# A convolution summed in PSUM, and weight low parts split between two engines, in a two-layer encoder trunk on one core

## The chip, the cores and the metric

The kernel runs as one program on one core of a Trainium2 chip. The metric is device time in microseconds (us), the median of 3 runs. The engines are named as in the profile: PE is the matrix engine (PEld its weight loads), DVE the vector engine, ACT the scalar engine, POOL is GpSimd, and SP issues most DMA transfers.

## What is computed

Two layers over a 256 x 2048 residual `h`, in float32:

```python
for i in range(DEPTH):                      # 2
    hn = _rmsnorm(h, norm_g[i])
    u = hn @ w_in[i]                        # 2048 -> 3*1024 + 1024 + 2*256 + 1024
    a_val, a_glu, a_z, q, k, v, b_z = jnp.split(u, offs, axis=-1)
    ya = _conformer_conv(a_val, a_glu, ...) # a = val*sigmoid(glu); depthwise conv, 31 taps;
                                            # layernorm over 1024 channels; silu
    ya = ya * jax.nn.silu(a_z)
    yb = _window_attention(q, k, v, bias_band, sink[i]) * jax.nn.silu(b_z)   # 16 heads
    h = h + jnp.concatenate([ya, yb], axis=-1) @ w_out[i]
    e = _rmsnorm(p[i] @ w_pe[i], pe_g[i])
    h = h + e * jax.nn.sigmoid(h @ w_pg[i])
return _rmsnorm(h, final_g)
```

## The kernel before

Everything is held transposed: channels on the 128 partitions, the 256 positions along the free axis. The weights stream from HBM in "halves" of 128 x 1024 numbers, two halves to a 1 MB transfer (`raw`, 3 buffers). Each matrix product is made of three products of the PE's rounded format, so every half is split first into a high part and a low part (`split`, L163 and L166): ACT casts `raw` to the high part, and DVE subtracts it from `raw` to give the low part. Both parts are one tile `w` (5 buffers); below, w9 is the tile of half 9. A half occupies PE with 24 matmuls of 256 columns: for each of 8 blocks high x high (L394), high x low of the activations (L395), and low x high (L396). L396 is the first that needs the low part. A layer has 154 halves, numbered from 0 in layer 0 and from 154 in layer 1; within a layer they serve `w_pe` (0 to 3), the convolution's value and gate columns `ag` (4 to 35), keys and values (36 to 43), attention gates and queries `zb`, `q` (44 to 75), the convolution's output gate `za` (76 to 91), then `w_out` and `w_pg`.

DVE, PE and ACT run their instructions in the order in which the program records them (`MAN`); POOL's are put in order by the scheduler. After each half `pump` records some convolution taps (about three, by `RATES`) and one piece of each side task. Halves are split four ahead of their use, but only two or so ahead in the first few halves of a layer, where halves come in pairs that PE uses interleaved (4 with 5, 6 with 7, 8 with 9, 10 with 11), while DVE still makes the normalised activations (`hn` L463, then `hg` L467).

The convolution of one tile of 128 channels (`conv`) is one ACT instruction for the middle tap and the bias (L553), and 30 multiply-adds on DVE (L560), each of which reads the input `a` and the sum `acc`, both in SBUF. Two tiles are worked on in turn, so that neighbouring instructions belong to different tiles. When a tile is done, POOL adds it to `ysum` (L565).

The side task `attention` runs for 8 pairs of heads, one after the other, while halves 54 to 91 are used: it loads its bias (`load_bias`, L334, a DMA that POOL issues), PE makes the scores (`sc`, L629), DVE adds the bias and takes the row limits (L635), ACT the exponentials (L642), DVE the denominators `den` (L646 and L647; both inputs of L646 are in SBUF), ACT scales (L650), PE transposes (`pt`, L656) and multiplies with the values (`av`, L666). Another side task, `embed`, has ACT square `e` (L380) and POOL add the squares to `eacc` (L381) during halves 16 to 31.

Of the kernel before, what the change touches and what calls it, by code (L numbers as in the profile page):

```python
# [10 lines left out]
F32 = mybir.dt.float32  # L11
F32R = mybir.dt.float32r
AF = mybir.ActivationFunctionType
ALU = mybir.AluOpType
PSUM = bass.MemoryType.PSUM
DRAM = bass.MemoryType.DRAM

P = 128
D = 2048
S = 256  # L20
# [10 lines left out]
PAD = TAPS // 2  # L31
# [17 lines left out]

NB_FIRST = 14  # L50
NSPL = 5
MAN = 'DVE,PE,Activation'
LY = (2, 1)
ORD = 1
AW = (0,0,0,0)
# [61 lines left out]
NHALF = len(HALVES)  # L117
# [3 lines left out]
PO_CW, PO_CB, PO_LG, PO_LB, PO_PE = 0, TAPS * NCT, (TAPS + 1) * NCT, (TAPS + 2) * NCT, (TAPS + 3) * NCT  # L121
# [4 lines left out]
def trunk_kernel(ctx: ExitStack, tc: tile.TileContext, xT, pT, wst, par, gain, relb, sinkp, onehot, out):  # L126
    nc = tc.nc
    ET = mybir.EngineType
    if MAN:
        ctx.enter_context(tc.manual_schedule(engines={getattr(ET, x) for x in MAN.split(",")}))  # L130
    big = ctx.enter_context(tc.tile_pool(name="big", bufs=5))
# [1 line left out]
    wspl = ctx.enter_context(tc.tile_pool(name="wspl", bufs=NSPL))  # L133
    cst = ctx.enter_context(tc.tile_pool(name="cst", bufs=1))
    wk = ctx.enter_context(tc.tile_pool(name="wk", bufs=2))
    ps = ctx.enter_context(tc.tile_pool(name="ps", bufs=8, space=PSUM))
    dram = ctx.enter_context(tc.tile_pool(name="dram", bufs=1, space=DRAM))

    def bigt(name, dt=F32):

        return big.tile([P, 2, 8, S], dt, tag="big", name=name)

    def halves(t):
        return [t[:, 0], t[:, 1]]
# [14 lines left out]
    def split(h):  # L159
        raw = raws[h // 2][:, h % 2, :]  # L160
        w = wspl.tile([P, 2, HALF], F32R, tag="w", name=f"w{h}")
        hi, lo = w[:, 0], w[:, 1]
        nc.scalar.copy(hi, raw)  # L163
        spl[h] = w
        if h not in (4, 5):
            nc.vector.tensor_sub(lo, raw, hi.bitcast(F32))  # L166

    def first_lo(h):

# [3 lines left out]
    def ahead(h):  # L173

        while state["spl"] < min(h, TOT - 1):
            n = state["spl"] + 1
            while state["raw"] < min(n // 2 + LD - 1, TOT // 2 - 1):
                state["raw"] += 1
                load(state["raw"])
            if HALVES[n % NHALF][0] != "w_pe" or n >= NHALF:  # L180
                split(n)
            state["spl"] = n

    def get(h):

        r = h % NHALF
        if r < 12:
            ahead(h + (r | 1) + 2 - r)
        else:
            ahead(h + LS)  # L190
        return spl.pop(h)
# [82 lines left out]
    h = halves(bigt("x"))  # L274
# [18 lines left out]
    def pcol(l, o):  # L293
        return pars[:, l * PW + o:l * PW + o + 1]
# [111 lines left out]
    class Cursor:  # L406
        h = 0
# [39 lines left out]
    for l in range(DEPTH):  # L447
# [27 lines left out]
        for q in range(4):  # L475
            n = Cursor.h
            Cursor.h += 1
            if l:
                w = get(n).rearrange("p t (j k c) -> p t j k c", j=4, k=2)
            else:  # L480
                raw = raws[n // 2][:, n % 2, :].rearrange("p (j k c) -> p j k c", j=4, k=2)
# [65 lines left out]
        a, acc = halves(bigt(f"ac{l}"))  # L547
# [2 lines left out]

        def conv(t, l=l, a=a, acc=acc, ysum=ysum, done=done):
            w = lambda k: pcol(l, PO_CW + t * TAPS + k)
            nc.scalar.activation(acc[:, t, :], a[:, t, :], AF.Identity, bias=pcol(l, PO_CB + t), scale=w(PAD))  # L553
            yield
            for k in range(TAPS):
                s = k - PAD
                if s == 0:
                    continue
                lo_, hi_ = max(0, -s), min(S, S - s)
                nc.vector.scalar_tensor_tensor(acc[:, t, lo_:hi_], a[:, t, lo_ + s:hi_ + s], w(k),  # L560
                                               acc[:, t, lo_:hi_], ALU.mult, ALU.add)
                yield
            done.append(t)
            if 2 <= len(done) <= NCT - 2:
                nc.gpsimd.tensor_add(ysum, acc[:, done[0], :] if len(done) == 2 else ysum, acc[:, t, :])  # L565

        def glu(t, b):
            u = wk.tile([P, S], F32, name=f"u{l}_{t}", tag="sg")
            nc.scalar.activation(u, b[:, 1, :], AF.Sigmoid)
            nc.vector.tensor_mul(a[:, t, :], b[:, 0, :], u)  # L570
            conv_q.append(conv(t))
# [27 lines left out]
        for q in range(4):  # L599
            n = Cursor.h  # L600
            Cursor.h += 1
            w = get(n).rearrange("p t (k c) -> p t k c", k=4)
            for kk in range(4):
                k = 4 * q + kk
# [66 lines left out]
        for i in range(0, 8, 2):  # L671
# [6 lines left out]
            for hh in range(2):  # L678
                r, o = rows_of[hh], rows_of[1 - hh]
# [158 lines left out]
        h = e  # L838
# [10 lines left out]
    for j in (0, 2, 12, 4, 6, 14, 8, 10):  # L849
        for x in [slice(0, 1), slice(1, 2)] if j == 0 else [slice(0, 2)]:  # L850
            d = og[j // 8][:, j % 8:j % 8 + 2, :][:, x, :]
            eng, r = (nc.gpsimd, rbs) if j >= 12 else (nc.vector, rb)
# [81 lines left out]
```

## Time and profile before

| | |
|---|---|
| median of 3 runs | 983.94 us (983.38 to 984.1) |
| the profiled execution's own time | 983.99 us |
| its span, first to last instruction | 982.2 us |
| mean granted PE clock | 0.992 |
| PE busy (matmuls) | 965.8 us, 98% of the span |
| PEld busy | 925.5 us, 94% |
| DVE busy | 774.6 us, 79% |
| ACT busy | 560.0 us, 57% |
| POOL busy | 86.6 us, 9% |

How to read it: busy time is the time in which an engine had an instruction under way, over one profiled execution. The page also follows a chain of work back from the last instruction, lists what each engine waited for, and shows stretches of the timeline row by row.

### The profile page before, as it was taken

How to read it: one execution, taken by the hardware profiler on the slowest of the kernel's cores; microseconds unless marked ns; L12 is line 12 of the kernel's file. 1: busy time of each engine (PE TensorE's matmuls, PEld its weight loads, DVE VectorE, ACT ScalarE, POOL GpSimd, SP SyncE). 2: the span in 40 equal slices, each digit the busy share in tenths (PEclk: the TensorE clock that was granted, in tenths of full speed). 3: DMA queues.
4: the chain of work that ended last, by engine and by line, in shares of the span. 5: the costliest groups of instructions: out<-in, count | busy, mean ns of one | idle time of the engine just before them, and what ended most of it. 6: DMA issues, size and time to landing. Idle time of an engine off the chain costs nothing.

```text
span 982.2 us, 18152 instructions
## 1 busy us (share of the span) xinstructions
PE 965.8 (98%) x7438; PEld 925.5 (94%) x7438; DVE 774.6 (79%) x1319; ACT 560.0 (57%) x862; POOL 86.6 (9%) x87
## 2 busy tenths in 40 slices
PE   8999999999999999999999999999999999999994
PEld 7999999999999999988899999999999999998884
DVE  4899989987787576687789998988887867667763
ACT  4655454777875554455566444568778545446551
POOL 0022001010000000011103200000100000100111
PEclk9999999999999999999999999999999999999997
DMA  7764636555544466446556555456454445654522
GB/s 287 254 238 171 213 131 215 189 178 181 166 153 177 149 238 225 172 172 230 198 184 237 175 203 181 172 188 204 146 168 165 172 143 200 217 191 162 197 104 86
DMA packets 29135, 182.49 MB, mean 186 GB/s; under 512 B 3723, under 2 KB 4284, under 8 KB 9212
## 3 DMA queue, kind: packets, MB, share of 16 engines
q1 hardware_dynamic: 24284, 165.17, 47.2%
q0 software_dynamic: 3472, 12.88, 4.4%
q10 hardware_dynamic: 1296, 3.28, 0.9%
q8 instruction: 58, 0.95, 0.4%
q14 instruction: 25, 0.20, 0.1%
HBM read 177.09 MB, written 4.23 MB: 185 GB/s over the span
## 4 chain that ended last, share of the span: by engine, by line
PE 97%; DVE 1%; DMA 1%; ACT 0%; POOL 0%; issue 0%; DVEq 0%; SPq 0%; ACTq 0%
PE g L391 12%; PE o L394 6%; PE o L395 6%; PE o L396 6%; PE ag L396 6%; PE ag L394 6%; PE ag L395 6%; PE g L392 6%; PE za L394 3%; PE zb L394 3%; PE q L394 3%; PE q L395 3%; PE zb L395 3%; PE za L395 3%; PE zb L396 3%; PE q L396 3%
## 5 line engine op out<-in xcount | busy, mean ns | idle before, releaser
L166 DVE TENSOR_TENSOR w<-raw,w 128x1024 fp32r<-128x1024 f32 x306 | 372.3, 1227 | 119.1 <-ACT w L163 116.1
L163 ACT CAST w<-raw 128x1024 fp32r<-128x1024 f32 x308 | 316.2, 1047 | 180.2 <-PE ag L396 45.1
L560 DVE SCALAR_TENSOR_TENSOR ac<-ac,pars 128x241 f32<-128x241 f32 (+11 forms) x480 | 217.9, 503 | 1.0
L391 PE MATMUL g<-h,w 128*128 128x512 f32 x496 | 175.3, 399 | 0.0
L396 PE MATMUL ag<-hg,w 128*128 128x256 f32 x512 | 145.2, 284 | 0.5 <-DVE w L166 0.5
L394 PE MATMUL ag<-hg,w 128*128 128x256 f32 x512 | 145.5, 284 | 0.0
L395 PE MATMUL ag<-hg,w 128*128 128x256 f32 x512 | 145.1, 283 | 0.1
L392 PE MATMUL g<-h,w 128*128 128x256 f32 x496 | 139.3, 281 | 0.0
L391 PEld LDWEIGHTS g<-h,w 128*128 128x128 f32 x496 | 93.2, 188 | 23.1
L394 PEld LDWEIGHTS ag<-hg,w 128*128 128x128 f32 x512 | 98.3, 192 | 0.9 <-ACT ac L553 0.9
L396 PEld LDWEIGHTS ag<-hg,w 128*128 128x128 f32 x512 | 98.3, 192 | 0.8 <-DVE w L166 0.7
L395 PEld LDWEIGHTS ag<-hg,w 128*128 128x128 f32 x512 | 98.3, 192 | 0.3 <-DVE hg L467 0.3
L392 PEld LDWEIGHTS g<-h,w 128*128 128x128 f32 x496 | 93.8, 189 | 0.0
L394 PE MATMUL za<-hg,w 128*128 128x256 f32 x256 | 73.7, 288 | 0.0
L394 PE MATMUL o<-yb,w 128*128 128x256 f32 x256 | 73.4, 287 | 0.0
L394 PE MATMUL q<-hg,w 128*128 128x256 f32 x256 | 73.3, 286 | 0.0
L394 PE MATMUL zb<-hg,w 128*128 128x256 f32 x256 | 73.2, 286 | 0.0
L395 PE MATMUL o<-yb,w 128*128 128x256 f32 x256 | 72.6, 284 | 0.0
L396 PE MATMUL o<-ya,w 128*128 128x256 f32 x256 | 72.5, 283 | 0.0
L394 PE MATMUL o<-ya,w 128*128 128x256 f32 x256 | 72.5, 283 | 0.0
L395 PE MATMUL o<-ya,w 128*128 128x256 f32 x256 | 72.5, 283 | 0.0
L396 PE MATMUL o<-yb,w 128*128 128x256 f32 x256 | 72.5, 283 | 0.0
(229 smaller groups left out, 2192.9 us busy)
## 6 DMA issues: line engine op xcount, KB each, us to landing
raw<-in_wst SPq DMA_DIRECT2D x153, 1024.0 KB, 4.9
bias<-fscr POOLq DMA_DIRECT2D x16, 384.0 KB, 3.8
raw<-in_wst SPq DMA_DIRECT2D x5, 512.0 KB, 9.8
x<-in_xT ACTq DMA_DIRECT2D x4, 512.0 KB, 7.1
hx<-in_xT POOLq DMA_DIRECT2D x8, 256.0 KB, 3.6
hscr<-e POOLq DMA_DIRECT2D x2, 1024.0 KB, 4.9
hx<-hscr POOLq DMA_DIRECT2D x8, 256.0 KB, 3.4
out_t<-og ACTq DMA_DIRECT2D x4, 256.0 KB, 3.0
```

The lines of the kernel that those rows point to most:

```text
L163: nc.scalar.copy(hi, raw)
L166: nc.vector.tensor_sub(lo, raw, hi.bitcast(F32))
L391: nc.tensor.matmul(o, w[:, 0], x, start=start, stop=False, skip_group_check=True)
L392: nc.tensor.matmul(o[:, 1], w[:, 1], x[:, 0], start=False, stop=stop, skip_group_check=True)
L394: nc.tensor.matmul(o, w[:, 0], x[:, 0], start=start, stop=False, skip_group_check=True)
L395: nc.tensor.matmul(o, w[:, 0], x[:, 1], start=False, stop=False, skip_group_check=True)
L396: nc.tensor.matmul(o, w[:, 1], x[:, 0], start=False, stop=stop, skip_group_check=True)
L560: nc.vector.scalar_tensor_tensor(acc[:, t, lo_:hi_], a[:, t, lo_ + s:hi_ + s], w(k), acc[:, t, lo_:hi_], ALU.mult, ALU.add)
```

## The change

The sums of the convolution move from `acc` (SBUF) to `y`, a half of one PSUM bank that is set aside for them: the two tiles in work use its two halves. The pool of PSUM banks that all else shares goes from 8 to 7. When a tile's taps are done, a new ACT copy brings `y` to `acc`. In halves 8 to 91 of each layer the low parts of three halves in four are made on POOL instead of DVE (63 subtractions a layer). And POOL joins the engines whose order is the program's.

```diff
-MAN = 'DVE,PE,Activation'
+MAN = 'DVE,PE,Activation,Pool'
...
-    ps = ctx.enter_context(tc.tile_pool(name="ps", bufs=8, space=PSUM))
+    ps = ctx.enter_context(tc.tile_pool(name="ps", bufs=7, space=PSUM))
+
+    cps = ctx.enter_context(tc.tile_pool(name="cps", bufs=1, space=PSUM))
+    ybank = cps.tile([P, 2, S], F32, name="y")
...
         nc.scalar.copy(hi, raw)
         spl[h] = w
         if h not in (4, 5):
-            nc.vector.tensor_sub(lo, raw, hi.bitcast(F32))
+            r = h % NHALF
+            (nc.gpsimd if 8 <= r < 92 and r % 4 else nc.vector).tensor_sub(lo, raw, hi.bitcast(F32))
...
         def conv(t, l=l, a=a, acc=acc, ysum=ysum, done=done):
             w = lambda k: pcol(l, PO_CW + t * TAPS + k)
-            nc.scalar.activation(acc[:, t, :], a[:, t, :], AF.Identity, bias=pcol(l, PO_CB + t), scale=w(PAD))
+            y = ybank[:, t % 2, :]
+            nc.scalar.activation(y, a[:, t, :], AF.Identity, bias=pcol(l, PO_CB + t), scale=w(PAD))
             yield
...
-                nc.vector.scalar_tensor_tensor(acc[:, t, lo_:hi_], a[:, t, lo_ + s:hi_ + s], w(k),
-                                               acc[:, t, lo_:hi_], ALU.mult, ALU.add)
+                nc.vector.scalar_tensor_tensor(y[:, lo_:hi_], a[:, t, lo_ + s:hi_ + s], w(k), y[:, lo_:hi_],
+                                               ALU.mult, ALU.add)
                 yield
+            nc.scalar.copy(acc[:, t, :], y)
             done.append(t)
```

What the change does to the order is seen at three places. The first is DVE at the opening of layer 0's projection, from the low part of half 8 on (w are the split tiles, hn and hg the activations). Before:

```order
L166 TENSOR_TENSOR w8_324<-raw4_201,w8_324 128x1024
L166 TENSOR_TENSOR w9_327<-raw4_201,w9_327 128x1024
L463 SCALAR_TENSOR_TENSOR hn_378<-x_84,gains_100,rh0b_211 128x256 x2
L463 SCALAR_TENSOR_TENSOR hn_382<-x_84,gains_100,rh0b_211 128x256 x2
L467 TENSOR_TENSOR hg0_1_311<-hn_378,hg0_1_311 128x512
L467 TENSOR_TENSOR hg0_1_311<-hn_382,hg0_1_311 128x512
L166 TENSOR_TENSOR w10_390<-raw5_251,w10_390 128x1024
L166 TENSOR_TENSOR w11_393<-raw5_251,w11_393 128x1024
```

and of the change:

```order
L170 TENSOR_TENSOR w8_328<-raw4_205,w8_328 128x1024
L467 SCALAR_TENSOR_TENSOR hn_382<-x_88,gains_104,rh0b_215 128x256 x2
L467 SCALAR_TENSOR_TENSOR hn_386<-x_88,gains_104,rh0b_215 128x256 x2
L471 TENSOR_TENSOR hg0_1_315<-hn_382,hg0_1_315 128x512
L471 TENSOR_TENSOR hg0_1_315<-hn_386,hg0_1_315 128x512
```

The low parts of halves 9, 10 and 11 are gone from DVE, and the activations follow w8 at once.

The second is POOL from the column of layer 0's first norm (rh0col) on. Before:

```order
L348 TENSOR_TENSOR rh0col_194<-rh0v_192,mhalf_114 128x2
L751 DMA hx_4032<-in_xT 128x512
L751 DMA hx_4034<-in_xT 128x512
L751 DMA hx_4092<-in_xT 128x512
L327 DMA fscr_128<-fs_553 16x511
L334 DMA bias0_1904<-fscr_128 128x2x384
L334 DMA bias1_2060<-fscr_128 128x2x384
L381 TENSOR_TENSOR eacc_132<-eacc_132,sq_686 128x512
```

and of the change:

```order
L352 TENSOR_TENSOR rh0col_198<-rh0v_196,mhalf_118 128x2
L170 TENSOR_TENSOR w9_331<-raw4_205,w9_331 128x1024
L170 TENSOR_TENSOR w10_394<-raw5_255,w10_394 128x1024
L170 TENSOR_TENSOR w11_397<-raw5_255,w11_397 128x1024
L170 TENSOR_TENSOR w13_456<-raw6_326,w13_456 128x1024
L170 TENSOR_TENSOR w14_519<-raw7_392,w14_519 128x1024
L170 TENSOR_TENSOR w15_522<-raw7_392,w15_522 128x1024
L331 DMA fscr_132<-fs_557 16x511
L170 TENSOR_TENSOR w17_563<-raw8_451,w17_563 128x1024
L170 TENSOR_TENSOR w18_596<-raw9_517,w18_596 128x1024
L170 TENSOR_TENSOR w19_627<-raw9_517,w19_627 128x1024
L385 TENSOR_TENSOR eacc_136<-eacc_136,sq_690 128x512
```

Low parts now fill POOL, and the early loads of the residual (hx) and of the first two biases have moved behind them, to the place where the program records them.

The third is DVE where it makes the first softmax denominators (den_1937 before, den_1945 of the change; ac0 and y are the convolution's sums), with the low part of half 60 ahead of them. Before:

```order
L560 SCALAR_TENSOR_TENSOR ac0_259<-ac0_259,pars_105 128x249
L560 SCALAR_TENSOR_TENSOR ac0_259<-ac0_259,pars_105 128x255
L166 TENSOR_TENSOR w60_2031<-raw30_1875,w60_2031 128x1024
L646 TENSOR_TENSOR den_1937<-den_1937,es_1938 128x4
L647 RECIPROCAL den_1937<-den_1937 128x4
L560 SCALAR_TENSOR_TENSOR ac0_259<-ac0_259,pars_105 128x250
```

and of the change:

```order
L565 SCALAR_TENSOR_TENSOR y_78<-ac0_263,pars_109,y_78 128x249
L565 SCALAR_TENSOR_TENSOR y_78<-ac0_263,pars_109,y_78 128x255
L170 TENSOR_TENSOR w60_2039<-raw30_1883,w60_2039 128x1024
L652 TENSOR_TENSOR den_1945<-den_1945,es_1946 128x4
L653 RECIPROCAL den_1945<-den_1945 128x4
L565 SCALAR_TENSOR_TENSOR y_78<-ac0_263,pars_109,y_78 128x250
```

Half 60's low part stays on DVE, directly ahead of the denominators; the taps read and write y instead of ac0, and half 61's low part is on POOL, beside them.

## Rows read from the trace of the kernel before

**Rows 1.** The page: busy time by engine, share of the span, instructions

```profile
PE 965.8 (98%) x7438; PEld 925.5 (94%) x7438; DVE 774.6 (79%) x1319; ACT 560.0 (57%) x862; POOL 86.6 (9%) x87
```

**Rows 2.** What PE waited for: total us, times, longest; five rows in all

```profile
PE e L490 <- DMA raw<-in_wst: 2.2, 1, 2.2
...
PE ag L396 <- DVE w L166: 0.5, 1, 0.5
```

**Rows 3.** Stretches: length; busy us of PE, PEld, DVE, ACT, POOL; clock

```profile
64.31:75.83 11.52, 11.52 (x99) 11.52 (x98) 11.52 (x18) 5.53 (x7) 4.02 (x3) 1.00 0.55 196
170.00:296.00 126.00, 126.00 (x1046) 121.08 (x1047) 106.20 (x240) 95.86 (x182) 8.54 (x10) 1.00 0.52 176
```

**Rows 4.** Groups by form: busy us, mean ns, idle before

```profile
L381 POOL TENSOR_TENSOR hacc<-hacc,sq 128x512 f32<-128x512 f32 x12 | 15.5, 1291 | 179.0 <-ACT sq L380 179.0
L463 DVE SCALAR_TENSOR_TENSOR hn<-x,gains,rh0b 128x256 f32<-128x256 f32 x16 | 6.7, 475 | 0.0
```

**Rows 5.** Timeline of POOL: start, us, instruction, idle before

```profile
162.25 0.81 POOL L565 TENSOR_TENSOR ysum<-ysum,ac 128x256 f32<-128x256 f32 x1 [7.42 <-DVE ac L560]
```

**Rows 6.** Timeline of ACT, DVE and POOL around two additions of POOL

```profile
86.66 1.70 POOL L381 TENSOR_TENSOR eacc<-eacc,sq 128x512 f32<-128x512 f32 x1 [4.73 <-ACT sq L380]
87.13 0.41 DVE L570 TENSOR_TENSOR ac<-ag,u 128x256 f32<-128x256 f32 x1
...
91.38 0.63 ACT L380 ACTIVATE sq<-e 128x512 f32<-128x512 f32 x1
92.15 1.53 POOL L381 TENSOR_TENSOR eacc<-eacc,sq 128x512 f32<-128x512 f32 x1 [3.79 <-ACT sq L380]
92.44 1.51 DVE L560 SCALAR_TENSOR_TENSOR ac<-ac,pars 128x249 f32<-128x249 f32 x1
```

**Rows 7.** Timeline at halves 8 to 11: ACT, DVE, PE

```profile
34.05 1.99 ACT L163 CAST w<-raw 128x1024 fp32r<-128x1024 f32 x2
35.13 2.36 DVE L166 TENSOR_TENSOR w<-raw,w 128x1024 fp32r<-128x1024 f32 x2 [0.26 <-ACT w L163]
37.84 0.28 PE L396 MATMUL ag<-hg,w 128*128 128x256 f32 x1
39.62 1.99 ACT L163 CAST w<-raw 128x1024 fp32r<-128x1024 f32 x2
43.60 0.28 PE L396 MATMUL ag<-hg,w 128*128 128x256 f32 x1
```

**Rows 8.** Timeline at halves 164 and 165 (8 and 9 of layer 1)

```profile
511.35 2.00 ACT L163 CAST w<-raw 128x1024 fp32r<-128x1024 f32 x2
515.24 0.28 PE L396 MATMUL ag<-hg,w 128*128 128x256 f32 x1
```

**Rows 9.** Timeline of DVE: two taps of one tile in a row

```profile
525.77 0.47 DVE L560 SCALAR_TENSOR_TENSOR ac<-ac,pars 128x242 f32<-128x242 f32 x1
526.27 0.47 DVE L560 SCALAR_TENSOR_TENSOR ac<-ac,pars 128x243 f32<-128x243 f32 x1
```

**Rows 10.** Timeline of the first attention of layer 0, from half 60's split

```profile
182.16 1.99 ACT L163 CAST w<-raw 128x1024 fp32r<-128x1024 f32 x2
183.23 1.22 DVE L166 TENSOR_TENSOR w<-raw,w 128x1024 fp32r<-128x1024 f32 x1 [1.23 <-ACT w L163]
184.37 0.15 DVE L646 TENSOR_TENSOR den<-den,es 128x4 f32<-128x4 f32 x1
184.83 1.71 ACT L650 ACTIVATE s<-s,den 128x256 f32<-128x256 f32 x4 [0.69 <-DVE den L647]
188.01 0.27 PE L656 MATMUL pt<-ident,s 128*128 128x128 f32 x1
```

**Rows 11.** Timeline of the last attention of layer 0

```profile
285.33 1.71 ACT L650 ACTIVATE s<-s,den 128x256 f32<-128x256 f32 x4 [0.69 <-DVE den L647]
288.71 0.27 PE L656 MATMUL pt<-ident,s 128*128 128x128 f32 x1
```

**Rows 12.** The page: DMA issues of POOL, KB each, us to landing

```profile
bias<-fscr POOLq DMA_DIRECT2D x16, 384.0 KB, 3.8
```

## The prediction

> **What bounds the kernel now.** I read the page's busy times first, then what PE waited for, then stretches of the timeline. PE is busy 98% of the span and its weight loads 94%, DVE 79%, POOL 9% [rows 1]. The list of PE's waits has five rows, of 2.2 us down to 0.5 [rows 2]; they lie at the start, in the first halves and at the very end. So from the first tiles of the projection to the last gate PE never stands still: four halves take 11.52 us, 2.88 each, all of it busy at the full granted clock [rows 3]. Nothing that relieves DVE can shorten that. The change can only leave PE's time alone or put gaps into it, and the work is to find where a low part or a result comes later than PE wants it.
>
> **The change part by part.**
>
> *Price of a subtraction on POOL.* The trace before has none of 128 x 1024. Left alone, POOL adds two 128 x 256 operands in 0.81 us [rows 5] and two 128 x 512 in 1.29 [rows 4]: 1.875 ns a column and 0.33 fixed, so 1,024 columns take 0.33 + 1.92 = 2.25 us, against 1.22 on DVE [rows 10]. Below, it could not be less than DVE's 1.22; above, 3.47, if each also stood behind one 1.22 us subtraction of DVE. I take 2.25, the line through POOL's own rows.
>
> *Who holds up whom.* DVE's tap that overlaps POOL's addition at 92.15 takes 1.51 us instead of 0.47: it stood still for 1.04, nearly all of a 512-column addition. Its two inputs are both in SBUF. The multiplication at 87.13, with one input in PSUM and one in SBUF, ran in 0.41 in the middle of another addition of POOL [rows 6]. So taps that read `y` in PSUM should run beside POOL, and what still collides with POOL are DVE's subtractions and other operations with both inputs in SBUF; one that loses to a low part on POOL waits up to its 1.92 us of columns.
>
> *Steady projection.* Three low parts are 6.75 us, with two additions to `eacc` (2.58) 9.3, in 11.52 us for four halves: hidden by the four halves of lead. Without that cover it costs the overflow, from 2.98 us a subtraction on while the squares run, from 3.84 elsewhere. DVE loses 63 x 1.22 = 77 us a layer.
>
> *Taps.* The two tiles now share a bank, so each tap follows the one just before it instead of the last but one. Dependent taps start 0.50 apart [rows 9], of which 0.47 is the tap. DVE has room: in 126 us it is busy 106.2 [rows 3], and sheds 24 x 1.22 = 29. That PSUM is written instead of SBUF is in no row; reading it costs nothing (`hn` with one operand in PSUM takes 475 ns [rows 4]). I take 0, with 0.36 more per tap as the bound: some 100 taps in that stretch would then eat the (126 - 106 + 29 - 12) us that stay free.
>
> *New copies, `ysum`, moved DMAs, one bank less.* An ACT copy per tile (8 a layer) and POOL's addition to `ysum` behind it now make POOL wait for the last tap, with the next low parts queued behind; the lead of 11.52 us covers some us of that, and ACT is busy 95.9 of 126 in its fullest stretch [rows 3]. The bias loads stand behind up to three low parts: 6.75 + 3.8 to land [rows 12] = 10.6, still inside the lead, and DVE wants them only after the scores. The residual's loads start with the first of 14 halves of `w_out`, 40 us before use. Seven banks suffice for `w_out`'s seven sums, and the norm's two small results come before the last of these is begun. All 0.
>
> *The opening of each projection: no cover.* Halves 8 to 11 are split just in time. The cast of w9 ends at 34.05 + 1.99 = 36.04; POOL starts 0.14 after ACT (91.38 + 0.63 to 92.15 [rows 6]); + 2.25 = 38.43. PE wants it at 37.84 [rows 7]: **0.6 late**. In layer 1: 511.35 + 2.00 + 0.14 + 2.25 = 515.74 against 515.24 [rows 8]: **0.5 late**. Nothing later gives this back, since PE has no slack after it. Then w10 and w11 follow each other on POOL: 40.6 + 0.14 + 4.5 = 45.2 against 43.60 [rows 7] + 0.6, 1.0 late if the casts stay; but the order shows `hn` right behind w8 on DVE, without w9's subtraction (1.1), and these casts follow the casts of `hg`. So they move up by as much: 0, with 1.0 a layer as the other end.
>
> *Softmax.* `den` stands right behind half 60's subtraction on DVE (183.23 + 1.22 = 184.45), and half 61's cast ends at 182.16 + 1.99 = 184.15 [rows 10]. So now POOL stands ready with w61 at 184.29 and takes over as DVE's subtraction ends; `den`, two inputs in SBUF, waits 1.92. ACT's scaling ended at 186.54, PE wanted it at 188.01: 1.47 to spare, **0.45 lost**. The last attention of the layer has 288.71 - 287.04 = 1.67 to spare [rows 11]: **0.25 lost**. The six between have more than one hold. 0.7 a layer, 1.4 in all, with 0 as the other end if the short operation slips in first. The Trainium skill, SBUF — State Buffer, section "Who interferes with whom", says that a vector instruction with two SBUF inputs and a GpSimd one that reads SBUF exclude each other for the whole instruction, whichever issues first. By that rule the loss is the full hold and the sum is the one below; by the row of the blocked tap alone, where a tap was the later one, an operation that is earlier would lose nothing and the sum is 985.0.
>
> *Sum.* 983.99 + 1.1 + 1.4 = 986.5 against the profiled execution, which is 0.05 over the median of 983.94: **986.4**.
>
> **The rivals.** What a measurement can tell from no change is about 0.2%, 1.97 us: 981.97 to 985.91.
>
> *Only the openings are late* (the other side: not slower). Place: `den` at halves 60 and 88. If DVE gets it done before POOL starts, the 1.4 falls away: 985.0. For it: the instruction takes 0.15 us. Against: w61 waits for the same moment. It decides from 0.77 us of softmax loss downward.
>
> *The change does nothing that PE sees.* It needs POOL to subtract in under 1.6 us, to be in time at 37.84: 983.9. Against it are both of POOL's rows; for it, only that no row has this shape.
>
> *POOL is the bottleneck of the openings.* At 3.47 a subtraction (the rounded output type dearer, or DVE in the way): w9 1.8, w165 1.7; the second pairs, with casts 1.1 earlier, 39.5 + 0.14 + 6.94 = 46.6 against 43.60 + 1.8, so 1.2 in each layer; softmax 1.4: 7.3 in all, 991.2. In the squares' stretch 3 x 3.47 + 2.58 = 13.0 in 11.52 adds a backlog of 6 over 16 halves, inside the lead. The Trainium skill, GPSIMD Engine Reference, section "Engine selection", keeps two-input elementwise work on VectorE, because GpSimd is about twice as slow. By twice DVE's 1.22 an estimate from that page is 2.45 us, 0.2 more at each opening, 986.8.
>
> *DVE late with taps or with a bias.* PSUM as target dearer by over 0.36 a tap, or a bias row that lands after its scores: every attention then stalls PE, 992 and more. Against it is DVE's free time.
>
> *Faster.* A wait of PE on DVE would have to vanish; the only one is 0.5 [rows 2], in the first halves, whose low parts the change leaves on DVE. Under 982 I see no path.
>
> **How the numbers follow.** Openings and softmax (985.6 to 987.8): 0.52, of which 0.43 over 985.91. Openings only: 0.20, same. Nothing: 0.06, same. POOL dear: 0.13, slower. Taps or bias late: 0.06, slower. Faster: 0.03. Together slower 0.62, same 0.35 and faster 0.03. The range runs from 984.5, just under the openings alone, to 991, the bound of POOL's price; the likeliest case's own is 985.6 to 987.8.
>
> **What would show it.** Right: POOL busy about 86.6 + 126 x 2.25 = 370 us; subtractions of 2.2 to 2.4; two new waits of PE (L400, on POOL) near 38 and 515, of about half a us; waits of PE at `pt` (L662), on ACT, near 188 and 289, and `den` starting some 2 us after the subtraction ahead of it; taps near 0.47, unblocked; DVE less busy by over 100 us. Wrong: subtractions over 3 us, waits of L400 all through the projection, scores waiting for bias, or PE's list of waits unchanged.

## The result, and the profile after

The changed kernel takes 988.84 us (median of 5 runs, 988.37 to 989.24), the kernel before 983.94 in the same series: a ratio of 1.0049, with a 95% interval of 1.0035 to 1.0063. It is slower by 4.9 us. The profiled execution took 989.24 us, with a span of 987.5 at a mean granted clock of 0.993; before, 983.99 and 982.2.

The page after, busy time by engine, to be read against [rows 1]:

```profile
PE 969.5 (98%) x7438; PEld 926.5 (94%) x7438; DVE 713.0 (72%) x1193; ACT 562.5 (57%) x878; POOL 383.4 (39%) x213
```

DVE lost 62 us and POOL gained 297, and PE is still busy 98% of a longer span. What PE waited for, after (total us, times, longest):

```profile
PE ag L400 <- POOL w L170: 1.3, 2, 0.7
...
PE pt L662 <- ACT s L656: 0.6, 2, 0.3
```

These two rows are new against [rows 2]: POOL's low part at L400, once in each layer's opening, and the scaled scores at the transposes `pt`, once in the fourth attention of each layer. Now the first opening, from ACT's, POOL's and PE's timelines, to be read against [rows 7]:

```profile
33.99 2.00 ACT L166 CAST w<-raw 128x1024 fp32r<-128x1024 f32 x2
36.06 2.48 POOL L170 TENSOR_TENSOR w<-raw,w 128x1024 fp32r<-128x1024 f32 x1 [16.29 <-ACT w L166]
38.60 0.39 PE L400 MATMUL ag<-hg,w 128*128 128x256 f32 x1 [0.68 <-POOL w L170]
38.41 2.00 ACT L166 CAST w<-raw 128x1024 fp32r<-128x1024 f32 x2
39.53 4.79 POOL L170 TENSOR_TENSOR w<-raw,w 128x1024 fp32r<-128x1024 f32 x2 [0.98 <-ACT w L166]
```

The cast of w9 ends where it did, POOL starts behind it and ends at 38.54, and PE, which wanted the low part at 37.84, goes on at 38.60. The casts of w10 and w11 moved from 39.62 up to 38.41, and POOL has both low parts done at 44.32, when PE is about to want them. In layer 1 the same matmul, at 515.24 before [rows 8], starts like this:

```profile
518.04 0.38 PE L400 MATMUL ag<-hg,w 128*128 128x256 f32 x1 [0.58 <-POOL w L170]
```

The second kind of loss is in the attentions. In the first one of layer 0, the rows of ACT, DVE, POOL and PE here answer to [rows 10]:

```profile
183.03 1.99 ACT L166 CAST w<-raw 128x1024 fp32r<-128x1024 f32 x2
184.10 1.23 DVE L170 TENSOR_TENSOR w<-raw,w 128x1024 fp32r<-128x1024 f32 x1 [3.35 <-ACT w L166]
185.11 2.48 POOL L170 TENSOR_TENSOR w<-raw,w 128x1024 fp32r<-128x1024 f32 x1 [4.22 <-ACT w L166]
185.25 2.36 DVE L652 TENSOR_TENSOR den<-den,es 128x4 f32<-128x4 f32 x1
187.91 1.71 ACT L656 ACTIVATE s<-s,den 128x256 f32<-128x256 f32 x4 [2.89 <-DVE den L653]
188.90 0.92 PE L662 MATMUL pt<-ident,s 128*128 128x128 f32 x5
191.92 1.15 DVE L645 TENSOR_TENSOR es<-nm,sinkt 128x4 f32<-128x4 f32 x1
```

`den`'s addition of 128 x 4 numbers takes 2.36 us instead of 0.15: it ends as POOL's subtraction ends, 2.2 later. ACT's wait for it grew from 0.69 to 2.89, and the next small addition of the same kind, `es`, is blocked as well.

The fourth attention loses most, and a second part of the change has a share in it, the new copy:

```profile
224.07 0.35 ACT L568 COPY ac<-y 128x256 f32<-128x256 f32 x1
224.97 0.57 ACT L558 ACTIVATE y<-ac,pars 128x256 f32<-128x256 f32 x1 [0.55 <-DVE y L565]
229.64 2.37 DVE L652 TENSOR_TENSOR den<-den,es 128x4 f32<-128x4 f32 x1
233.62 0.33 PE L662 MATMUL pt<-ident,s 128*128 128x128 f32 x1 [0.32 <-ACT s L656]
```

Before, ACT ran the next tile's first tap there as soon as the exponentials were done:

```profile
222.67 0.59 ACT L553 ACTIVATE ac<-ac,pars 128x256 f32<-128x256 f32 x1
```

Now ACT makes the copy (0.35 us) and then waits 0.55 for a tap of DVE, and the scaled queries `qq` and the casts that stand behind in its order are 0.9 later for it. `den` starts at 229.64 instead of 227.33, which is 0.97 more than PE's own lag of 1.34, and the hold of 2.2 comes on top. An estimate from these rows: before, the second scaled tile ended at 228.70 and PE took it up at 231.79; PE now takes it up 0.46 behind its end, so there were 2.6 us to spare. The hold alone (2.2) or the copy and its wait alone (0.9) would have fitted into that; together they do not.

Over the whole span the groups read so (busy us, mean ns, idle before):

```profile
L170 POOL TENSOR_TENSOR w<-raw,w 128x1024 fp32r<-128x1024 f32 x126 | 310.4, 2475 | 191.7 <-ACT w L166 187.5
L170 DVE TENSOR_TENSOR w<-raw,w 128x1024 fp32r<-128x1024 f32 x180 | 234.1, 1314 | 133.6 <-ACT w L166 130.7
L565 DVE SCALAR_TENSOR_TENSOR y<-ac,pars,y 128x241 f32<-128x241 f32 (+11 forms) x480 | 229.8, 479 | 35.0 <-ACT ac L568 11.2 <-ACT y L558 10.1
L652 DVE TENSOR_TENSOR den<-den,es 128x4 f32<-128x4 f32 x16 | 33.3, 2084 | 0.0
```

POOL's price is 2475 ns; the taps keep 479 beside all of it; `den` has a mean of 2084. In the projection's steady stretch and in that of the attentions [rows 3] PE stays busy:

```profile
64.31:75.83 11.52, 11.52 (x98) 11.52 (x97) 10.59 (x17) 5.53 (x8) 11.52 (x7) 1.00 0.68 247
172.00:298.00 126.00, 125.66 (x1037) 119.96 (x1037) 100.04 (x212) 93.86 (x181) 71.26 (x36) 1.00 0.49 174
```

To see where the 4.9 us lie I set the start of each matmul of PE after against the same matmul before. PE runs in the same order in both, so that the lag only grows where something came late:

| place | layer 0: before, after | lag | layer 1: before, after | lag |
|---|---|---|---|---|
| w9's first low product | 37.84, 38.60 | 0.76 | 515.24, 518.04 | 2.80 |
| the second pair | 43.72, 44.60 | 0.88 | 521.12, 524.04 | 2.92 |
| `pt`, first attention | 188.23, 189.27 | 1.04 | 664.49, 667.57 | 3.08 |
| second | 202.75, 204.05 | 1.29 | 679.00, 682.35 | 3.34 |
| fourth | 231.79, 233.62 | 1.82 | 708.04, 711.93 | 3.88 |
| eighth | 289.04, 291.01 | 1.97 | 765.29, 769.31 | 4.01 |
| start of `w_out` | 306.70, 308.82 | 2.12 | 782.96, 787.13 | 4.18 |

The lags are taken from unrounded times. The openings cost 0.88 + 0.81 = 1.69 us, the softmax 1.08 + 1.09 = 2.17, the starts of `w_out` 0.31. By its last matmul PE is 4.5 behind: some 0.4 come in the last norm, where the granted clock fell earlier (0.50 in the 2 us from 973.5 on, against 0.88 in the 2 us from 969 before). The stretch from there to the end of the span is 0.7 longer than before. That makes the 5.3 us of the spans.

### The profile page after: what moved, and what is told of

It is laid out like the page before. It is cut to its first block, busy times and chain, and to the rows that moved or that the text cites. A ratio compares the mean times of both kernels' runs of the same rounds, so it can differ in the third digit from the quotient of the medians.

```text
span 987.5 us, 18241 instructions
## 1 busy us (share of the span) xinstructions
PE 969.5 (98%) x7438; PEld 926.5 (94%) x7438; DVE 713.0 (72%) x1193; ACT 562.5 (57%) x878; POOL 383.4 (39%) x213
## 4 chain that ended last, share of the span: by engine, by line
PE 82%; ACT 8%; DVE 4%; issue 3%; DMA 1%; POOL 1%; DVEq 0%; SPq 0%; ACTq 0%; POOLq 0%
PE g L395 12%; PE o L399 6%; PE o L398 6%; PE o L400 6%; PE g L396 6%; PE ag L400 5%; PE ag L398 5%; PE ag L399 5%; PE za L398 3%; PE za L399 3%; PE za L400 3%; ACT w L166 2%; DVE den L652 2%; ACT s L648 2%; PE q L398 2%
## 5 line engine op out<-in xcount | busy, mean ns | idle before, releaser
L170 POOL TENSOR_TENSOR w<-raw,w 128x1024 fp32r<-128x1024 f32 x126 | 310.4, 2475 | 191.7 <-ACT w L166 187.5
L170 DVE TENSOR_TENSOR w<-raw,w 128x1024 fp32r<-128x1024 f32 x180 | 234.1, 1314 | 133.6 <-ACT w L166 130.7
L565 DVE SCALAR_TENSOR_TENSOR y<-ac,pars,y 128x241 f32<-128x241 f32 (+11 forms) x480 | 229.8, 479 | 35.0 <-ACT ac L568 11.2
L400 PE MATMUL ag<-hg,w 128*128 128x256 f32 x512 | 145.4, 284 | 1.8 <-POOL w L170 1.3
L400 PEld LDWEIGHTS ag<-hg,w 128*128 128x128 f32 x512 | 97.7, 191 | 2.5 <-POOL w L170 1.7
L385 POOL TENSOR_TENSOR hacc<-hacc,sq 128x512 f32<-128x512 f32 x12 | 15.5, 1291 | 187.7 <-ACT sq L384 187.7
L398 PE MATMUL o<-yb,w 128*128 128x256 f32 x256 | 73.3, 287 | 0.0
L399 PE MATMUL o<-yb,w 128*128 128x256 f32 x256 | 72.7, 284 | 0.0
L400 PE MATMUL o<-ya,w 128*128 128x256 f32 x256 | 72.5, 283 | 0.0
L399 PE MATMUL o<-ya,w 128*128 128x256 f32 x256 | 72.5, 283 | 0.0
```

The lines of the kernel that those rows point to most:

```text
L170: (nc.gpsimd if 8 <= r < 92 and r % 4 else nc.vector).tensor_sub(lo, raw, hi.bitcast(F32))
L385: (eng or nc.gpsimd).tensor_add(acc, acc, sq)
L398: nc.tensor.matmul(o, w[:, 0], x[:, 0], start=start, stop=False, skip_group_check=True)
L399: nc.tensor.matmul(o, w[:, 0], x[:, 1], start=False, stop=False, skip_group_check=True)
L400: nc.tensor.matmul(o, w[:, 1], x[:, 0], start=False, stop=stop, skip_group_check=True)
L565: nc.vector.scalar_tensor_tensor(y[:, lo_:hi_], a[:, t, lo_ + s:hi_ + s], w(k), y[:, lo_:hi_], ALU.mult, ALU.add)
```

## Experiments

Three theories were on trial. The **port theory**: the loss is the late low parts of the openings and the waits of `den` while POOL holds something that DVE needs for two SBUF inputs. The **copy theory**: ACT's new copies wait for taps in ACT's order, and ACT's work behind them is late. The **bank theory**: seven PSUM banks are too few somewhere. Each ratio is to the kernel before, run on the same chip.

### POOL starts at half 12

```diff
-            (nc.gpsimd if 8 <= r < 92 and r % 4 else nc.vector).tensor_sub(...)
+            (nc.gpsimd if 12 <= r < 92 and r % 4 else nc.vector).tensor_sub(...)
```

> POOL takes over low parts from half 12 of each layer on instead of half 8. Port theory (the loss is 1.7 us in the openings, where POOL's subtraction is not ready in time, and 2.2 us at the softmax, where the denominators on DVE wait for POOL's subtraction to let go of the shared port): PE's two waits for POOL vanish, the delay of 0.8 to 0.9 us at each opening goes to 0.1 or less, the delays at pt stay (1.1 us a layer), and the time falls by 1.7 us to about 987.1. Copy theory (the softmax loss comes from ACT's new copies and from its first taps, which wait in ACT's order for DVE's taps): the same for the openings. Bank theory (one PSUM bank less costs PE waits): no change in the openings.

986.8 us, 1.0030 (1.0019 to 1.0042), 2.0 under the changed kernel. PE's waits for POOL are gone, and the matmul of w9 starts at 37.84 as before. The lags at `pt` are all still there and sum to 2.2. The openings are worth what the table says.

### Two of four from half 44 on

```diff
-            (nc.gpsimd if 8 <= r < 92 and r % 4 else nc.vector).tensor_sub(...)
+            (nc.gpsimd if 8 <= r < 92 and (r % 4 if r < 44 else r % 4 > 1) else nc.vector).tensor_sub(...)
```

> From half 44 on POOL makes two low parts of four (the third and fourth) instead of three, so that none starts while DVE is about to add up the denominators; halves 8 to 43 as in the change. Port theory: den at 0.15 us in most of the 16 places, delays at pt under 0.3 us a layer, openings as they were: about 986.7. Copy theory: copies, taps and their waits are unchanged, so the delays at pt stay: 988.5.

987.52 us (986.54 to 988.24), 1.0035 (1.0023 to 1.0048), 0.8 over the 986.7 that was expected. Half 61, whose subtraction POOL took up ahead of `den`, is DVE's again, as is the second of every four halves from 44 on. The tile's row shows that no addition is blocked now (least, median and longest ns):

```profile
L652 DVE TENSOR_TENSOR den<-den,es x16: 155/155/158, 187.4 to 763.4; 128x4 f32<-128x4 f32 x16
```

All lags at `pt` are gone, the openings' remain.

### den's addition on ACT

```diff
-            nc.vector.tensor_add(den, den, es)
+            for b, hh in each:
+                d = den[:, b, hh:hh + 1]
+                nc.scalar.activation(d, es[:, b, hh:hh + 1], AF.Identity, bias=d, scale=1.0)
```

> As the changed kernel, but the sink's part is added to den by four small Identity activations of ScalarE (bias from den) instead of VectorE's 128x4 addition of two SBUF tensors. Port theory, which has 2.2 us of the loss in that addition's waits for GpSimd's subtractions: they go, and ScalarE's four small operations cost little of it back, 986.5 to 987.4. Rival (den is only the place where VectorE's general lateness shows, and the wait moves to the reciprocal or to the next step): 988.3 to 989.2, with the same delays at pt.

985.77 us, 1.0020 (1.0011 to 1.0029): 3.1 under the changed kernel, more than expected. ACT's rows of the first attention (in this execution PE runs 2.4 us later from the first weights on):

```profile
186.43 0.84 ACT L654 ACTIVATE den<-es,den 128x1 f32<-128x1 f32 x4
188.12 1.71 ACT L658 ACTIVATE s<-s,den 128x256 f32<-128x256 f32 x4
```

Four activations take 0.84 us of ACT, and the scaling starts without a wait. The lags at `pt` are gone and those at the start of `w_out` too, though POOL still makes three of four low parts; so these were a consequence of `den`'s waits. The 3.1 are 2.2 at `pt`, 0.3 at `w_out` and 0.6 behind the last DMA issue. The edit also puts ACT's cast of half 61 behind the activations, so POOL starts that subtraction later; the run does not separate the two, but together with the run before it shows that the softmax loss needs the meeting of `den` and POOL. The copy and its wait of 0.55 are still in ACT's order at the fourth attention, and without the hold PE is not late there.

### Both repairs

```diff
-            (nc.gpsimd if 8 <= r < 92 and r % 4 else nc.vector).tensor_sub(...)
+            (nc.gpsimd if 12 <= r < 92 and r % 4 else nc.vector).tensor_sub(...)
...
-            nc.vector.tensor_add(den, den, es)
+            (the four activations as above)
```

> As the changed kernel, three of four low parts by GpSimd, with both repairs: it starts at half tile 12 of a layer (986.8 alone) and den's addition is on ScalarE (985.77 alone). Port theory, which has the whole loss of PE in the openings and in den's waits: both kinds of delay are gone and PE's matmuls run as in the kernel before but for 0.3 us, 983.8 to 984.9 with up to 0.7 us of the longer end in it. Rival (PSUM taps, copies, seven banks or the order have a price of their own that the two edits don't touch): 985.5 or more.

983.98 us, 0.9999 (0.9990 to 1.0009): the time of the kernel before, with 120 low parts on POOL. The page and PE's waits:

```profile
PE 964.8 (98%) x7438; PEld 924.1 (94%) x7438; DVE 688.8 (70%) x1183; ACT 574.4 (59%) x942; POOL 368.9 (38%) x207
```

```profile
PE ag L400 <- DVE w L170: 0.5, 1, 0.5
```

Neither of the two new rows of PE's waits is left. The copies, the seventh bank, GpSimd's order and the taps in PSUM are all still in this kernel, so with POOL's help they cost nothing that can be measured by themselves; the bank theory falls, and so does the copy theory as a cause of its own. The share of the copy in the fourth attention, on top of `den`'s hold, was not tried apart: no run takes the copies away and leaves the hold. It is no gain either: PE was the bound and still is, with DVE relieved by 86 us.

### Late start and two of four

```diff
-            (nc.gpsimd if 8 <= r < 92 and r % 4 else nc.vector).tensor_sub(...)
+            (nc.gpsimd if 12 <= r < 92 and (r % 4 if r < 44 else r % 4 > 1) else nc.vector).tensor_sub(...)
```

> As the changed kernel, but GpSimd starts at half tile 12 of a layer instead of 8, and from half tile 44 on it takes two of four instead of three. Port theory, which has the loss in the openings (1.7 us) and in den's waits (2.2 us) and nothing besides: both go, what is left is some 0.3 to 1 us, 984.2 to 985.6. Copy theory and bank theory: the copies and the seven banks are still there, 986.5 or more.

985.06 us, 1.0011 (1.0002 to 1.0020), as expected. PE's lag, apart from the first 10 us, is 0.26; 0.7 of the rest lies behind the last matmul.

### The same, half of the copies on DVE

```diff
-            nc.scalar.copy(acc[:, t, :], y)
+            (nc.vector.tensor_copy if t % 2 else nc.scalar.copy)(acc[:, t, :], y)
```

> As the kernel that starts at half tile 12 and takes two of four later (985.06), but the convolution's copies out of PSUM are made by VectorE for the odd tiles, which takes 16 instructions from ScalarE's program. In the kernels with ScalarE's program at 1218 recorded instructions an instruction transfer lies 2.8 us before the end and the time from the last DMA issue to the end is 6.2 us; in those with 1214 or fewer it is 5.5 and there is no such transfer. Program length theory: the 0.7 us at the end go, 984.0 to 984.5. Rival (the late transfer has another cause, GpSimd's work for one): the end stays at 6.2 us, 984.8 to 985.3.

984.40 us, 1.0000 (0.9991 to 1.0009). In the changed kernel and five of its variants an instruction transfer runs some 3 us before the end, beside the last output transfers, and the time from the last DMA issue to the end is 5.9 to 6.3 us; in the others, and before, 5.4 to 5.6. The last 4 us of the changed kernel and of the one with both repairs, by the queue list of each window (packets, MB, share):

```profile
q14 instruction: 2, 0.02, 1.0%
```

```profile
q14 instruction: 1, 0.01, 0.5%
```

The count of ACT's recorded instructions came to 1220 here and not below 1218, since the split adds waits; the transfer is still there and the end is 5.9. So the edit did not test what it was made for. That some 0.3 to 0.9 us of the end go with this transfer is seen in all 14 kernels; whose instructions it brings, and that it is the cause, stays open.

### All low parts on DVE

```diff
-            (nc.gpsimd if 8 <= r < 92 and r % 4 else nc.vector).tensor_sub(...)
+            nc.vector.tensor_sub(...)
```

> All low parts back on DVE; the convolution in its PSUM bank, seven banks for the rest and POOL in program order stay. Port theory: nothing of PE's gaps is left, within 0.5 us of the kernel before, 984. Copy theory: the softmax loss stays or grows, 986 or more, with waits of PE at pt for ACT. Bank theory: PE waits for PSUM stay, 986 or more.

992.08 us, 1.0077 (1.0063 to 1.0091): taking POOL's work away makes it 3.2 worse, which the port theory did not foresee. PE's waits have another first row:

```profile
PE sc L635 <- DVE qq L687: 3.9, 4, 1.1
```

The scaled queries `qq` stand in DVE's order behind the taps, and DVE comes to them late. Its timeline ahead of them:

```profile
169.35 1.50 DVE L565 SCALAR_TENSOR_TENSOR y<-ac,pars,y 128x247 f32<-128x247 f32 x3
...
171.90 1.50 DVE L565 SCALAR_TENSOR_TENSOR y<-ac,pars,y 128x242 f32<-128x242 f32 x3
173.43 0.68 DVE L687 SCALAR_TENSOR_TENSOR qq<-q,qq 64x512 fp32r<-64x512 f32 x1
```

Three taps now take 1.50 us, against 1.23 in the kernel with the order alone (below), where `qq` starts at 167.98. DVE is 173.43 - 167.98 = 5.45 late there. Of these, 1.1 are PE's own lag in this execution, there since the first weights (before 13 us), and 1.1 more are two waits of DVE for ACT's copy and first tap (0.64 at 158.29, 0.49 at 167.26). PE waits 1.1 and 0.9. What follows is in the windows of this kernel, for layer 0 and then for the same place in layer 1; behind the busy times stands the granted clock:

```profile
173.00:176.70 3.70, 1.71 (x13) 1.48 (x13) 2.63 (x4) 2.53 (x4) 0.00 (x0) 1.00 0.74 249
176.70:180.20 3.50, 3.50 (x20) 3.50 (x19) 3.36 (x7) 1.00 (x2) 0.00 (x0) 0.52 0.08 35
...
653.00:656.50 3.50, 1.56 (x11) 1.15 (x10) 2.40 (x5) 1.86 (x3) 0.00 (x0) 1.00 0.82 290
656.50:660.50 4.00, 4.00 (x35) 4.00 (x35) 3.90 (x6) 2.25 (x3) 0.00 (x0) 1.00 0.04 16
```

Behind the stretch in which PE was busy 1.71 of 3.70 us the clock is granted at 0.52, the 1.2 GHz level, for 3.5 us; that costs another 1.5. In layer 1 PE was busy 1.56 of 3.50 us, with waits of the same 1.1 and 0.85, and the clock stayed full. From 1.1 the lag grows to 5.1 at the scores of layer 0, and to 8.2 by the end, 2.5 of it at the scores of layer 1.

### POOL only in the first 36 halves

```diff
-            (nc.gpsimd if 8 <= r < 92 and r % 4 else nc.vector).tensor_sub(...)
+            (nc.gpsimd if 8 <= r < 44 and r % 4 else nc.vector).tensor_sub(...)
```

> POOL makes low parts only in halves 8 to 43 of each layer; while attention runs, all low parts are on DVE. Port theory: den (L652) takes 0.15 us again instead of 2.36, no delay at pt, the openings keep their 1.7 us; about 986.2 to 986.7. Copy theory: the copies and their waits are all still there and DVE is busier, so the delays at pt stay at 1 us a layer or grow; 988.8 or more. Bank theory: 988.8.

994.31 us, 1.0104 (1.0090 to 1.0118), 8 us over what the port theory expected. No lag at `pt`, but the openings' stay, and PE waits 3.8 us for `qq` again, as long as with all low parts on DVE, with the lower clock behind it in both layers: what DVE has to do between half 44 and the first scores is enough to make it late, whatever POOL has done before.

### The order alone

```diff
-MAN = 'DVE,PE,Activation'
+MAN = 'DVE,PE,Activation,Pool'
```

> The kernel before with GpSimd in program order as the one edit: eight banks, taps in SBUF, every low part by VectorE. Tap theory (what made the kernel with all low parts on VectorE 8 us slower are the PSUM taps, which start 0.50 us apart instead of 0.39): the order costs nothing, 983.5 to 984.5. Order theory (GpSimd's work comes later in program order and somebody waits for it): part or all of the 8 us is here, 986 to 992.

This is the kernel before with one edit: 984.03 us, 1.0002 (0.9993 to 1.0011). The order costs nothing by itself. Its taps, in SBUF, ahead of `qq`:

```profile
166.72 1.23 DVE L560 SCALAR_TENSOR_TENSOR ac<-ac,pars 128x242 f32<-128x242 f32 x3
167.98 0.68 DVE L681 SCALAR_TENSOR_TENSOR qq<-q,qq 64x512 fp32r<-64x512 f32 x1
```

### Half of the tiles in PSUM

```diff
-            y = ybank[:, t % 2, :]
+            y = ybank[:, 1, :] if t % 2 else acc[:, t, :]
...
-            nc.scalar.copy(acc[:, t, :], y)
+            if t % 2:
+                nc.scalar.copy(acc[:, t, :], y)
```

on top of all low parts on DVE.

> As the kernel with all low parts on VectorE (992.08), but only the odd tiles accumulate in the PSUM bank, the even ones in SBUF as before, so that taps alternate between the two places and half of the copies go. Chain theory (a tap waits for the tap before it since both work on one bank): the starts of alternating taps are 0.39 us apart again, VectorE keeps up as before, 984 to 985.5. Access theory (a tap with an operand and the output in PSUM takes its 0.50 whatever stands ahead of it): the spacing alternates, 0.50 behind a PSUM tap and 0.39 behind an SBUF tap, half of VectorE's delay goes, 986 to 989. Copy theory (the loss is in the waits for ScalarE's copy): half of these go, 987 to 989, with taps 0.50 apart.

984.01 us, 1.0002 (0.9993 to 1.0011): the whole 8 us are gone. DVE's timeline:

```profile
166.81 0.47 DVE L565 SCALAR_TENSOR_TENSOR y<-ac,pars,y 128x242 f32<-128x242 f32 x1
167.19 0.47 DVE L565 SCALAR_TENSOR_TENSOR ac<-ac,pars 128x249 f32<-128x249 f32 x1
167.58 0.47 DVE L565 SCALAR_TENSOR_TENSOR y<-ac,pars,y 128x243 f32<-128x243 f32 x1
168.08 0.68 DVE L688 SCALAR_TENSOR_TENSOR qq<-q,qq 64x512 fp32r<-64x512 f32 x1
```

Taps that alternate between the bank and SBUF start 0.38 to 0.39 apart, behind either kind. So it is not PSUM as a target that costs: it is two neighbouring taps in one bank, 0.50 apart, for the greater part. The other part may be the copies: DVE's two waits for ACT's copy and first tap (1.1 us together) are gone here as well, although half of the copies are still made, and the run does not separate the two. Whether the program's tracking of the bank as one tile or the bank itself holds the second back was not tried.

### The convolution back in SBUF

```diff
-    ps = ctx.enter_context(tc.tile_pool(name="ps", bufs=7, space=PSUM))
-
-    cps = ctx.enter_context(tc.tile_pool(name="cps", bufs=1, space=PSUM))
-    ybank = cps.tile([P, 2, S], F32, name="y")
+    ps = ctx.enter_context(tc.tile_pool(name="ps", bufs=8, space=PSUM))
...
-            y = ybank[:, t % 2, :]
+            y = acc[:, t, :]
...
-            nc.scalar.copy(acc[:, t, :], y)
```

> As the changed kernel, but the convolution accumulates in SBUF as before (eight banks, no copy behind the taps); GpSimd's low parts and its program order stay. Port theory: a tap then reads two SBUF inputs, as den's addition does, and waits for whole subtractions of GpSimd; the mean of L560's taps goes from 479 ns to over 600, DVE falls behind in the projection, qq comes late at the turn to attention, and the time is 992 to 1000. Copy theory and bank theory: ScalarE's copies and the seventh bank were the cost, so the time falls to 984 to 987 and the taps stay at 480 to 500 ns.

1051.62 us, 1.0687 (1.0672 to 1.0701), far beyond what was expected, in the direction of the port theory. The taps and PE's waits:

```profile
L563 DVE SCALAR_TENSOR_TENSOR ac<-ac,pars 128x241 f32<-128x241 f32 (+11 forms) x480 | 381.3, 853 | 2.3 <-ACT ac L556 0.9
```

```profile
PE ag L398 <- DVE w L168: 20.7, 4, 8.5
PE sc L632 <- DVE qq L684: 7.2, 4, 3.1
```

With both inputs in SBUF a tap takes 853 ns in the mean, DVE is busy 864.7 us instead of 713.0, and PE waits for it everywhere. The move to PSUM is what makes POOL's part possible at all.

### POOL scheduled

```diff
-MAN = 'DVE,PE,Activation,Pool'
+MAN = 'DVE,PE,Activation'
```

> As the changed kernel, but without GpSimd in program order: its loads of bias and hx then stand ahead of subtractions that now stand ahead of them. Port theory: the same subtractions meet the same steps, 988.3 to 989.3. Order theory (a load that waits for its buffer holds the subtractions behind it): over 990, with waits for GpSimd's low parts at L398 to L400 at new places.

998.21 us, 1.0149 (1.0135 to 1.0162). It is over 990, but not because a load held subtractions behind it. POOL's and DVE's timelines:

```profile
67.47 2.42 POOL L170 TENSOR_TENSOR w<-raw,w 128x1024 fp32r<-128x1024 f32 x1
69.83 1.30 POOL L385 TENSOR_TENSOR eacc<-eacc,sq 128x512 f32<-128x512 f32 x1
71.08 4.75 POOL L170 TENSOR_TENSOR w<-raw,w 128x1024 fp32r<-128x1024 f32 x2
75.78 1.26 POOL L385 TENSOR_TENSOR eacc<-eacc,sq 128x512 f32<-128x512 f32 x1
77.00 2.34 POOL L170 TENSOR_TENSOR w<-raw,w 128x1024 fp32r<-128x1024 f32 x1
65.53 14.90 DVE L170 TENSOR_TENSOR w<-raw,w 128x1024 fp32r<-128x1024 f32 x1
```

One subtraction of DVE with two SBUF inputs stood through these six operations of POOL and the end of one before them, 14.90 us instead of 1.22, and PE waited 5.3 us for it, with the lower clock behind the wait. In the changed kernel POOL is as busy here, and DVE's subtraction at the same place has its turn as soon as the one subtraction under way has ended:

```profile
64.55 3.38 DVE L170 TENSOR_TENSOR w<-raw,w 128x1024 fp32r<-128x1024 f32 x1
```

What differs is that two bias loads stand between POOL's subtractions just ahead (POOL issues the second at 66.71); that these took DVE's turn was not tried. They are not needed for it: in layer 1 of this run a subtraction of DVE, from 532.99 on, took 5.83 us through three operations of POOL with no load between them. By the same starts of matmuls the stall with its lower clock makes 7.3 of the 9.4 us to the changed kernel; the rest is in the openings, where loads of `hx` now stand between the subtractions of w9 and w10. So the order edit, free by itself, is needed once POOL has the subtractions.

## Why the prediction was right, and where not

The forecast was 986.4 us and the result 988.84, inside the range and on the forecast side; both places of the loss were named with their causes, and both are shown by the runs that repair them. The size was not met: 2.5 us of loss were forecast and 4.9 measured, above the 985.6 to 987.8 that the prediction gave this case. That the result lies inside the range is owed to the rival with a dear subtraction, which set the upper end and did not come. By the spans, where 5.3 us are missing, the openings take 0.6 more than forecast, the softmax 0.8, the starts of `w_out` 0.3, the last norm 0.4 and the end 0.7.

*Openings.* Forecast 0.6 and 0.5, measured 0.76 and 0.69 at the low product of w9. The matmul right behind it comes 0.10 later still (in layer 0 at 38.82 instead of 37.96, a lag of 0.86), which stood in no term; the second pair, taken at 0 with 1.0 as the other end, adds only 0.02. The step that was mis-sized is **the price of a subtraction on POOL**: 2.48 us at w9, not 2.25, of which POOL's earlier start (0.07 behind the cast, not 0.14) gave a part back. The straight line through POOL's two additions was too low by a tenth; the prediction's other estimate, 2.45, was nearer. At w9 POOL's first 0.2 us lie beside the end of DVE's own subtraction of w8. The shift of the second pair's casts, read from the order, came as said.

*Softmax.* Forecast 0.7 a layer, measured 1.08 and 1.09. The mechanism was right: POOL takes over as DVE's subtraction ends, ahead of the `den` that DVE wants next. The Trainium skill, SBUF — State Buffer, section "Who interferes with whom", says that a vector instruction with two SBUF inputs and a GpSimd one that reads SBUF exclude each other for the whole instruction; the 2.36 us of `den` agree. **"The six between have more than one hold"** is the step that failed: the loss lies in the first, second, fourth and eighth attention (0.22, 0.24, 0.54 and 0.08 in layer 0, from the matmul ahead of `pt` to the fourth transpose), and two of the six lose most of it. The second had less to spare because a late scaling makes ACT's next casts and exponentials late: they start at 193.77 instead of 191.54, 2.2 later where PE's own lag is 1.1. At the fourth the exponentials are on time (1.4 later, with PE's lag at 1.34), and it is the copy and its wait, priced at nothing in another paragraph, that use up the spare time ahead of `den`. Both were read from the trace and not tried apart. The first and the last lose less than forecast (0.22 and 0.08 instead of 0.45 and 0.25), since PE's transposes start with the first scaled tile and do not wait for the fourth.

*Starts of `w_out`, the last norm and the end.* 0.3, 0.4 and 0.7 us stood in no term. The first vanishes with `den`'s waits; the second goes with the clock of this execution; the third is open.

*Taps at nothing, since DVE has room.* The number came true, the reason only half. The spacing of 0.50 was foreseen. But the room was read in the stretch of the attentions; in the projection DVE was busy all of 11.52 us [rows 3], and ahead of the first scores the room is what POOL makes: with all low parts on DVE the convolution in its bank costs 8 us, most of it at these scores. The bound of 0.36 more per tap looked at the wrong stretch: with DVE as full as that, 0.11 per tap with the waits for the copies was enough.

*Copies, `ysum`, loads, seven banks.* All 0 by the run with both repairs. In the changed kernel itself the copies are not free: the term looked at ACT's busy time and not at what ACT waits for, and at the fourth attention the copy and its wait take 0.9 us of the spare time that `den`'s hold needs. The bias loads now land after 6.0 us instead of 3.8 [rows 12], hidden as forecast.

*What would show it.* Of the list, POOL's busy time (383 for 370) and its subtractions (2475 ns, for 2.2 to 2.4) were a little over; the waits near 38 and 515 (517 on the later clock of this run) and `den`'s delay came as written; PE's waits at `pt` came in the fourth attentions, near 233 and 712, and not near 188 and 289, where the delay is too small for the list; the taps stayed at 0.48. DVE was to be less busy by over 100 us and was by 62: DVE's instructions that wait for POOL count as busy, 31 us more in `den` alone, 16 in the low parts that stayed and 8 in `es`; the taps add 12. A sum was off as well: the softmax loss that decides for the rival of the openings alone is 985.91 - 983.94 - 1.1 = 0.87, not 0.77; nothing hangs on it.

## What to carry to other kernels

In this kernel work moved to GpSimd was paid for where VectorE next touched two SBUF operands, however small the operation was (2.36 us for 128 x 4): look up what stands right behind each place where GpSimd becomes ready, and move that operation to another engine or leave that one piece on VectorE. A copy that is new in an engine's order is to be priced by what it waits for, at the place with the least to spare, and not by the engine's busy time. Where a result is split just in time, leave it on the faster engine until there is a lead. And accumulations that alternated between two tiles lost their overlap when both tiles became halves of one bank (0.50 us apart instead of 0.39); on an engine that was nearly full, that was most of what made the next stage late.

## What was not expected of the hardware

A VectorE instruction that meets GpSimd mostly waits for one instruction, the 2.2 us of `den`. In a few cases it waited through more: 14.90 us through six, 5.83 through three in the same run, and in the run with the convolution back in SBUF a tap, from 58.10 on, 11.63 through five. The Trainium skill, SBUF — State Buffer, section "Who interferes with whom", speaks of the one whole instruction; no run here shows what lets the next one go first.

Not only operations with two SBUF inputs are held. In the changed kernel the negation of 128 x 32 numbers, with one SBUF input, took this long, and 0.18 us before:

```profile
54.64 2.37 DVE L326 TENSOR_SCALAR nsink<-sinkt 128x32 f32<-128x32 f32 x1
```

The same section of the Trainium skill counts `tensor_scalar` among the operations that can take the shared ports in a two-port mode; the trace agrees with a hold, and does not show the mode. So a single SBUF input was not the safe side that the prediction took it for. It cost nothing here, since nothing waits for `nsink` until the scores.

With all low parts on DVE, PE's granted clock fell to the 1.2 GHz level behind waits of 1.1 and 0.85 us close together in layer 0, and did not behind the same two waits in layer 1; with POOL only in the first 36 halves it fell in both layers. It fell behind a wait of 5.3 with POOL scheduled, but not behind the single waits of 0.7 and 0.6 in the changed kernel's openings. Two waits that sum to 2.0 us cost 4.0 where the clock fell and 2.5 where it did not.
